# A hybrid decoder block on one Trainium2 core: the last key and query sums of each recurrence half placed behind the newest bank add on VectorE

## The chip, the core and the metric

The kernel runs on one core of a Trainium2 chip. Five engines work side by side, each on its own list of instructions in program order: TensorE (PE in the profile; its weight loads are PEld), VectorE (DVE), ScalarE (ACT), GpSimd (POOL) and SyncE (SP), which issues most of the transfers. They wait for each other through semaphores. Matmuls write into PSUM, here eight banks of 128 x 512 fp32 values; the other engines read a bank out, or add it onto a tile in SBUF.

The metric is the device time of one execution in microseconds. The kernel before took 1442.57 us (median of three runs, 1440.68 to 1442.67).

## The reference, cut to what matters

```
proj = x @ w_in -> [q | f | i | og | pool_v | gate_a | gate_b]
a = HGRN2(q, f, i) -> per-head RMSNorm * sigmoid(og) -> @ w_a
b = per-group linear(causal_mean_w(pool_v) - pool_v) * pool_scale
mix = (sigmoid(gate_a) * a + sigmoid(gate_b) * b) @ w_out
x = LN(alpha * x + mix);  x = LN(alpha * x + relu(x @ w_up)^2 @ w_down)

# HGRN2, per head, in chunks:
G = cumsum(log_f);  q_dec = q * exp(G);  k_inv = k * exp(-G);  k_to_end = k * exp(G_last - G)
scores = tril(q_dec @ k_inv^T);  o = scores @ v + q_dec @ state
state  = exp(G_last) * state + k_to_end^T @ v
```

All of it is fp32, with 1024 tokens, a width of 1024, 8 heads of 128 and one layer. What the change touches lies in the HGRN2 part: the products of the keys and queries with their decays.

## The kernel before, in words

**The products.** Every fp32 operand is split into a rounded high part and the rest, and each block product is three matmuls of 128 x 512 (high by high, high by rest, rest by high: lines 213, 215 and 216 in `prod`). The products with `w_in` run by a seven-product scheme for 2 x 2 blocks: `pair` makes one such group of seven products of 12 matmuls each. A weight block becomes its two parts by a cast on ScalarE (line 250) and a subtraction on VectorE (line 251); the sums of weight blocks that the scheme needs are made on VectorE too (lines 303, 320, 328, 335).

**Bank adds.** The seven products of a group go into three PSUM banks. Where a bank holds a sum that belongs to two outputs, ScalarE copies it to a tile (`copied`, line 294) and VectorE later adds a bank onto that tile (`added`, line 298: the *bank add*, which writes a tile named `c` or `f`). In the order used through the recurrence (p1, p2, p6, p7, p5, p4, p3) the bank called `a` is read by the bank add after p5, and p3 goes on adding to the same bank. Between p5 and p3 stands one product on another bank, p4. So p3 cannot start before that bank add is done.

**The recurrence beside the products.** Each of the 8 heads is done in two halves of 512 tokens; this text numbers the halves 0 to 15. For each half `Half.prepare` makes the scaled keys and queries in pieces on VectorE, ScalarE and GpSimd; then come the transposes of `ke` (`turn_keys`, line 1069), the scores (line 1076), the states and the outputs. The pieces are run by `recurrence`, a generator; after each product of the projections (`run` and `run_ahead`) one step of it is taken, so the recurrence's work is spread between the products. Some 8.25 products go to one half.

The last two pieces of `prepare` make, for one half: `q` times a decay for odd blocks of 16 (line 1049), `kr` likewise for even blocks (line 1050; the tile is called `tE`), `ke` = `kr` times `ek` (line 1052; tile `tC`), and `q64` and `k64` for the far scores by 32 keys: of each, one half is copied on ScalarE (lines 1057, 1060) and the other multiplied on VectorE (lines 1058, 1061). Right after them `far_queries` makes `tA` from `q` (line 1096).

**What sets the order.** PE's order through this stage is as the program is written. On the other engines a scheduler with its own estimate of times sets the order at build time, within the dependences. `tc.issue_after(i)` is one more bound: what is written inside it stands behind instruction `i` on the same engine's list. It is no wait on a semaphore. The kernel uses it already as `behind_act`: the copies to `q64` and `k64` stand behind the newest ScalarE instruction of a product's result (`last_act`).

Names in the rows of the order: `tE` is `kr`, `tC` is `ke`, `tA` is `far_queries`' result or a running decay product, `raw` is a weight block or a sum of such, `w` a weight part, `pA` and `pC` are running sums of the causal pooling, `st` the state, `ps_pj` a bank of a projection product, `T` and `p32` decays.

Of the kernel before, what the change touches and what calls it, by code (L numbers as in the profile page):

```python
# [16 lines left out]
P = 128  # L17
# [6 lines left out]
CH = HALF // P  # L24
SUB = 16
NB = HALF // SUB
# [26 lines left out]
def tile_hybrid_block(  # L53
# [19 lines left out]
    V, A, G, PE = nc.vector, nc.scalar, nc.gpsimd, nc.tensor  # L73
# [16 lines left out]
    def nm(s):  # L90
        seq[0] += 1
        return f"{s}_{seq[0]}"
# [7 lines left out]
    def ps_tile(tag="pj", bufs=4):  # L100
        if tag == "hg":
            hg_tags.append(hg_tags.pop(0))
            tag, bufs = hg_tags[-1], 1
        return pp.tile([P, HALF], F32, tag=tag, name=nm("ps_" + tag), bufs=bufs)
# [76 lines left out]
    def minus_sum(out, a, b):  # L181
        V.scalar_tensor_tensor(out, a, -1.0, b, ALU.mult, ALU.subtract)
# [25 lines left out]
    def prod(ps, w, name, first):  # L208
        wh, wl = w
        for k in range(CH):  # L210
            th, tl = xp[name][k][:, 0], xp[name][k][:, 1]
            with tc.high_priority(PRIO_WHOLE) if k else nullcontext():
                PE.matmul(ps, wh[:, k], th, start=first and k == 0, stop=False, skip_group_check=True)  # L213
            with tc.high_priority(PRIO_WHOLE):
                PE.matmul(ps, wh[:, k], tl, start=False, stop=False, skip_group_check=True)  # L215
                PE.matmul(ps, wl[:, k], th, start=False, stop=k == CH - 1, skip_group_check=True)  # L216

    def block_tile(shape=(CH, P)):
        return wq.tile([P, *shape], F32, tag="raw", name=nm("raw"), bufs=6)
# [23 lines left out]
    def w_tile():  # L243
        return wq.tile([P, CH, P], F32R, tag="w", name=nm("w"), bufs=NW)

    hi_of, lo_of, last_act = [], [], [None]

    def w_part(src):
        hi, lo = w_tile(), w_tile()
        hi_of.append(A.copy(hi, src).ins)  # L250
        lo_of.append(V.tensor_sub(lo, src, f(hi)).ins)  # L251
        return hi, lo
# [7 lines left out]
    def noted(i):  # L260
        last_act[0] = i.ins
        return i

    def behind_act():
        return tc.issue_after(last_act[0])

    n_c = [0]

# [17 lines left out]
    def pair(raw, rooms, takes, pz_tag="pj", twin=False, pc_tag="pj", turned=False):  # L286


        b11, b12, b21, b22, t = raw if len(raw) == 5 else (*raw, None)
        c, ps = {}, {}  # L290

        def copied(room, ps):
            t = room()
            noted(A.copy(t, ps))  # L294
            return t

        def added(t, ps):
            V.tensor_add(t, t, ps)  # L298
            return t

        def make_t3():
            c["t"] = block_tile() if t is None else t
            V.tensor_sub(c["t"], b22, b12)  # L303

        def t3():
            if twin:
                make_t3()
            return w_part(c["t"])

        def t2():  # L310
            if not twin:
                make_t3()
                make_t2()
            return w_part(b12)

        def make_t2():
            if turned:
                minus_sum(b12, c["t"], b11)
            else:
                V.tensor_add(b12, c["t"], b11)  # L320

        def t4():
            if twin:
                make_t2()
            if turned:
                minus_sum(b21, b12, b21)
            else:
                V.tensor_sub(b21, b21, b12)
            return w_part(b21)

        def t1():
            if turned:
                minus_sum(c["t"], b22, b12)
            else:
                V.tensor_sub(c["t"], b22, b12)
            return w_part(c["t"])

        def p1(w):
            ps["a"] = ps_tile()
            prod(ps["a"], w, "a11", True)  # L340
            c[11] = copied(rooms[0], ps["a"])

        def p2(w):
            if pz_tag == "pj":
                ps["z"] = ps_tile()
            ps["c"] = ps_tile(pc_tag, 4 if pc_tag == "pj" else 2)
            prod(ps["c"], w, "a12", True)

        def p7(w):
            if pz_tag != "pj":  # L350
                ps["z"] = ps_tile(pz_tag, 2)
            prod(ps["z"], w, "s3", True)
            with tc.high_priority(PRIO):
                takes[0](added(c[11], ps["c"]))
                c[22] = copied(rooms[2], ps["z"])

        def p6(w):
            prod(ps["a"], w, "s2", False)
            with tc.high_priority(PRIO):
                c[21] = copied(rooms[1], ps["a"])  # L360
                if twin:
                    takes[2](added(c[21], ps["z"]))

        def p4(w):
            prod(ps["z"], w, "a22", False)
            if not twin:
                with tc.high_priority(PRIO):
                    takes[2](added(c[21], ps["z"]))

        def p5(w):  # L370
            prod(ps["a"], w, "s1", False)
            with tc.high_priority(PRIO):
                takes[3](added(c[22], ps["a"]))

        def p3(w):
            prod(ps["a"], w, "s4", False)
            with tc.high_priority(PRIO):
                takes[1](ps["a"])

        def t0():  # L380
            return w_part(b11)

        def b_21():
            return w_part(b21)

        def b_22():
            return w_part(b22)

        middle = (
            ((t3, p7), (t4, p4), (t2, p6), (t1, p5)) if twin else ((t2, p6), (t3, p7), (t1, p5), (t4, p4))  # L390
        )
        return tuple(
            ((operand,), ((operand, product),)) for operand, product in ((t0, p1), (b_21, p2), *middle, (b_22, p3))
        )
# [66 lines left out]
    with tc.tile_pool(name="xr", bufs=8, side="right", reuse_waits="tile") as xr:  # L461
# [5 lines left out]
        ps = ps_tile("hg", 2)  # L467
# [274 lines left out]
    with tc.tile_pool(name="tmp", bufs=1, side="right", reuse_waits="tile") as tmp:  # L742
# [15 lines left out]
        def tt(tag, dtype=F32):  # L758
            pool = tmp if tag in ("q", "f", "og", "v") else hgp
            return pool.tile([P, HALF], dtype, tag=tag, name=nm(tag), bufs=RINGS.get(tag, 1))  # L760

        def small(tag, shape, bufs=2):
            n = math.prod(shape[1:])
            t = hgp.tile([P, max(n, LINE)], F32, tag=tag, name=nm(tag), bufs=bufs)[:, :n]
            return t if len(shape) == 2 else t.rearrange("p (a b) -> p a b", b=shape[2])
# [204 lines left out]
        def pairs_of(t):  # L970
            return t.rearrange("p (b e s) -> p b e s", e=2, s=SUB)

        def half64(t, e):
            return t.rearrange("p (c e b s) -> p c e b s", e=2, b=2, s=2 * SUB)[:, :, e]

        def bc(a, shape):
            return a.unsqueeze(len(a.shape)).to_broadcast(shape)
# [4 lines left out]
        def b32(t):  # L982
            return t.rearrange("p (b s) -> p b s", s=32)

        class Half:
# [4 lines left out]
            def prepare(self):  # L990

                h, u = self.h, self.u
                ft, q = inputs[h][0][u], inputs[h][1][u]
# [4 lines left out]
                to_end = tt("tC")  # L998
# [14 lines left out]
                T2 = T.rearrange("p (b e) -> p b e", e=2)  # L1013
                p32 = small("p32", [P, CH, 4])
# [12 lines left out]
                ek = small("ek", [P, CH, 4])  # L1027
# [7 lines left out]
                with behind_act():  # L1035
                    A.activation(k, ft, AF.Identity, bias=cmask[:, P - 1 : P], scale=-1.0)
# [4 lines left out]
                with behind_act():  # L1041
                    A.copy(pairs_of(kc)[:, :, 0], pairs_of(kr)[:, :, 0])
                V.tensor_mul(pairs_of(kc)[:, :, 1], pairs_of(kr)[:, :, 1], bc(rT2[:, :, 1], [P, NB // 2, SUB]))
                self.qc = qc = tt("tF")
                with behind_act():
                    A.copy(pairs_of(qc)[:, :, 1], pairs_of(q)[:, :, 1])
                V.tensor_mul(pairs_of(qc)[:, :, 0], pairs_of(q)[:, :, 0], bc(rT2[:, :, 0], [P, NB // 2, SUB]))
                yield
                V.tensor_mul(pairs_of(q)[:, :, 1], pairs_of(q)[:, :, 1], bc(T2[:, :, 0], [P, NB // 2, SUB]))
                V.tensor_mul(pairs_of(kr)[:, :, 0], pairs_of(kr)[:, :, 0], bc(T2[:, :, 1], [P, NB // 2, SUB]))  # L1050
                self.ke = ke = to_end
                V.tensor_mul(b32(ke), b32(kr), bc(ek.rearrange("p c b -> p (c b)"), [P, 16, 32]))
                yield
                self.q64 = q64 = hgp.tile([P, CH, 2, 32], F32, tag="q64", name=nm("q64"))
                self.k64 = k64 = hgp.tile([P, CH, 2, 32], F32, tag="k64", name=nm("k64"))
                with behind_act():
                    A.copy(q64[:, :, 0], half64(q, 1)[:, :, 0])
                V.tensor_mul(q64[:, :, 1], half64(q, 1)[:, :, 1], bc(p32[:, :, 2], [P, CH, 32]))
                with behind_act():
                    A.copy(k64[:, :, 1], half64(kr, 0)[:, :, 1])  # L1060
                V.tensor_mul(k64[:, :, 0], half64(kr, 0)[:, :, 0], bc(p32[:, :, 1], [P, CH, 32]))
                self.q = q

            def turn_keys(self):
# [521 lines left out]
    for b in range(NBLK):  # L1586
# [3 lines left out]
        if last:  # L1590

            for ring in (dh, dw):
                t = fw.tile([P, M, 2, HALF], F32R, tag="draw", name=nm("dx"), bufs=2)
                ring[:0] = [(t[:, n], t[:, n + 1]) for n in (0, 2)]
        for i, (name, slot, chain, fresh, (u, nh)) in enumerate(steps):
# [13 lines left out]
            for c in range(CH):  # L1609
                t = u * CH + c  # L1610
# [10 lines left out]
    for i, c in ((0, 0), (0, 1), (1, 0), (1, 1), (0, 2), (1, 2), (0, 3), (1, 3)):  # L1621
        _, _, chain, fresh, (_, nh) = ends[i]
        ps = down_tile(ops[i], chain, fresh, c)
# [36 lines left out]
```

## Time and profile before

| | |
|---|---|
| median of three runs | 1442.57 us (1440.68, 1442.57, 1442.67) |
| time of the profiled execution | 1440.68 us |
| its span, first to last instruction | 1439.0 us |
| busy: PE, DVE, ACT, POOL | 1424.9, 1099.3, 753.6, 108.6 us |
| mean granted TensorE clock | 0.998 |
| recurrence beside the projections | about 113 to 546 us of the span |

A row of the timeline gives the start in us, the duration in us, engine, line, operation, output and inputs, the shape, and in brackets the idle time of the engine before it with what ended it. Instructions of VectorE and ScalarE overlap a little at their ends, so what an instruction takes of its engine is the distance from its start to the next start. Matmuls overlap by almost half; there too the distance of starts counts. A row of a table by stretches gives the stretch, its length, the busy time (and count) of PE, PEld, DVE, ACT and POOL, the granted clock, the transfer engines' share and GB/s.

### The profile page before, as it was taken

How to read it: one execution, taken by the hardware profiler on the slowest of the kernel's cores; microseconds unless marked ns; L12 is line 12 of the kernel's file. 1: busy time of each engine (PE TensorE's matmuls, PEld its weight loads, DVE VectorE, ACT ScalarE, POOL GpSimd, SP SyncE). 2: the span in 40 equal slices, each digit the busy share in tenths (PEclk: the TensorE clock that was granted, in tenths of full speed). 3: DMA queues.
4: the chain of work that ended last, by engine and by line, in shares of the span. 5: the costliest groups of instructions: out<-in, count | busy, mean ns of one | idle time of the engine just before them, and what ended most of it. 6: DMA issues, size and time to landing. Idle time of an engine off the chain costs nothing.

```text
span 1439.0 us, 21137 instructions
## 1 busy us (share of the span) xinstructions
PE 1424.9 (99%) x7499; PEld 1184.6 (82%) x7499; DVE 1099.3 (76%) x1816; ACT 753.6 (52%) x1376; POOL 108.6 (8%) x296
## 2 busy tenths in 40 slices
PE   9999999999999999999999999999999999999997
PEld 7888888888888888878888888888888888888886
DVE  5967887897797796579965697666666787777978
ACT  5445566666656655456532375555556443433534
POOL 0002011111211210100003000000000100000000
PEclk9999999999999999999999999999999999999999
DMA  7142254444454546799651225444456864444422
GB/s 271 62 137 91 87 131 148 109 128 145 110 125 132 142 124 189 214 325 348 190 205 64 99 66 189 155 161 161 149 180 245 292 243 146 149 141 167 133 73 117
DMA packets 186794, 228.17 MB, mean 159 GB/s; under 512 B 12192, under 2 KB 110784, under 8 KB 186688
## 3 DMA queue, kind: packets, MB, share of 16 engines
q1 hardware_dynamic: 180080, 210.94, 44.0%
q0 software_dynamic: 5824, 13.63, 4.5%
q10 hardware_dynamic: 784, 2.25, 0.5%
q8 instruction: 59, 0.97, 0.3%
q14 instruction: 47, 0.39, 0.1%
HBM read 149.70 MB, written 77.07 MB: 158 GB/s over the span
## 4 chain that ended last, share of the span: by engine, by line
PE 94%; DVE 3%; DMA 1%; issue 1%; ACT 1%; DVEq 0%; POOL 0%; ACTq 0%; SPq 0%; POOLq 0%
PE ps_pj L213 16%; PE ps_pj L215 16%; PE ps_pj L216 16%; PE ps_pj L1539 4%; PE ps_pj L1538 4%; PE ps_pj L1537 4%; PE ps_pj L115 2%; PE ps_pj L116 2%; PE ps_pj L114 2%; PE ps_tr L1539 2%; PE ps_tr L1538 2%; PE ps_tr L1537 2%; PE ps_hg L216 1%; PE ps_sc L213 1%; PE ps_sc L216 1%; PE ps_hg L213 1%
## 5 line engine op out<-in xcount | busy, mean ns | idle before, releaser
L213 PE MATMUL ps_pj<-act,w 128*128 128x512 f32 x1068 | 420.1, 393 | 2.7 <-DVE c L298 2.4
L215 PE MATMUL ps_pj<-act,w 128*128 128x512 f32 x1068 | 415.4, 389 | 0.0
L216 PE MATMUL ps_pj<-act,w 128*128 128x512 f32 x1068 | 415.1, 389 | 0.0
L250 ACT CAST w<-raw 128x512 fp32r<-128x512 f32 x303 | 187.7, 621 | 260.6 <-PE ps_pj L215 179.9
L251 DVE TENSOR_TENSOR w<-raw,w 128x512 fp32r<-128x512 f32 x303 | 207.1, 686 | 95.8 <-ACT w L250 93.3
L213 PEld LDWEIGHTS ps_pj<-act,w 128*128 128x128 f32 x1068 | 200.6, 188 | 46.1 <-DVE c L298 3.7
L216 PEld LDWEIGHTS ps_pj<-act,w 128*128 128x128 f32 x1068 | 200.5, 188 | 42.2
L215 PEld LDWEIGHTS ps_pj<-act,w 128*128 128x128 f32 x1068 | 200.6, 188 | 40.4
L1499 ACT CAST act<-act 128x1024 fp32r<-128x1024 f32 x66 | 67.1, 1050 | 108.4 <-issue 35.0
L1538 PE MATMUL ps_pj<-act,act 128*128 128x512 f32 x240 | 93.1, 389 | 0.0
L1539 PE MATMUL ps_pj<-act,act 128*128 128x512 f32 x240 | 93.1, 389 | 0.0
L1500 DVE TENSOR_TENSOR act<-act,act 128x1024 fp32r<-128x1024 f32 x66 | 79.4, 1219 | 17.4 <-ACT act L1499 17.4
L1537 PE MATMUL ps_pj<-act,act 128*128 128x512 f32 x240 | 92.6, 389 | 0.0
L298 DVE TENSOR_TENSOR c<-c,ps_pj 128x512 f32<-128x512 f32 x91 | 62.1, 683 | 33.4 <-PE ps_pj L216 32.3
L294 ACT COPY c<-ps_pj 128x512 f32<-128x512 f32 x92 | 53.3, 581 | 3.3 <-PE ps_pj L216 1.8
L1538 PEld LDWEIGHTS ps_pj<-act,act 128*128 128x128 f32 x240 | 45.1, 188 | 9.5 <-DVE act L1500 0.2
L1537 PEld LDWEIGHTS ps_pj<-act,act 128*128 128x128 f32 x240 | 45.1, 188 | 9.4
L1539 PEld LDWEIGHTS ps_pj<-act,act 128*128 128x128 f32 x240 | 45.1, 188 | 9.3
L303 DVE TENSOR_TENSOR raw<-raw,raw 128x512 f32<-128x512 f32 x43 | 29.6, 688 | 24.6 <-DMA raw<-in_w_in_dram 19.7
L1408 ACT ACTIVATE c<-c 128x512 f32<-128x512 f32 x61 | 38.5, 633 | 1.7
L1407 ACT ACTIVATE c<-c 128x512 f32<-128x512 f32 x46 | 29.0, 632 | 16.3 <-DVE c L298 16.3
L737 POOL DMA_DIRECT2D s<-og x28 | 24.9, 1162 | 137.1 <-DVE og L1150 137.1
(432 smaller groups left out, 2706.4 us busy)
## 6 DMA issues: line engine op xcount, KB each, us to landing
h<-c SPq DMA_DIRECT2D x106, 256.0 KB, 2.9
raw<-in_w_in_dram SPq DMA_DIRECT2D x100, 256.0 KB, 3.3
act<-h SPq DMA_DIRECT2D x78, 256.0 KB, 2.9
draw<-in_w_down_dram SPq DMA_DIRECT2D x16, 1024.0 KB, 8.2
raw<-in_w_up_dram SPq DMA_DIRECT2D x56, 256.0 KB, 2.9
hf<-h SPq DMA_DIRECT2D x34, 256.0 KB, 2.9
s<-og POOLq DMA_DIRECT2D x28, 256.0 KB, 6.0
v<-v SPq DMA_DIRECT2D x16, 256.0 KB, 3.4
```

The source lines that it names most:

```text
L213: PE.matmul(ps, wh[:, k], th, start=first and k == 0, stop=False, skip_group_check=True)
L215: PE.matmul(ps, wh[:, k], tl, start=False, stop=False, skip_group_check=True)
L216: PE.matmul(ps, wl[:, k], th, start=False, stop=k == CH - 1, skip_group_check=True)
L250: hi_of.append(A.copy(hi, src).ins)
L251: lo_of.append(V.tensor_sub(lo, src, f(hi)).ins)
L294: noted(A.copy(t, ps))
L298: V.tensor_add(t, t, ps)
L1499: A.copy(hi, src)
L1500: V.tensor_sub(lo, src, f(hi))
L1537: PE.matmul(ps, hh[:, w], wh, start=fresh and n == 0, stop=False, skip_group_check=True)
L1538: PE.matmul(ps, hh[:, w], wl, start=False, stop=False, skip_group_check=True)
L1539: PE.matmul(ps, hl[:, w], wh, start=False, stop=n == M - 1, skip_group_check=True)
```

## The change

`added` now notes its bank add in `last_add`, and `behind_add` places what is written inside it behind the newest bank add. The last VectorE products of `prepare` stand inside it: lines 1049, 1050 and 1052 in one piece, lines 1058 and 1061 in the next. The two ScalarE copies stand together. What is computed, and the count of instructions, stay the same. The line numbers behind line 246 move by 3, and from here on by 4 to 5 behind the changed piece.

```diff
-    hi_of, lo_of, last_act = [], [], [None]
+    hi_of, lo_of, last_act, last_add = [], [], [None], [None]
...
+    def behind_add():
+        return tc.issue_after(last_add[0])
...
         def added(t, ps):
-            V.tensor_add(t, t, ps)
+            last_add[0] = V.tensor_add(t, t, ps).ins
             return t
...
-                V.tensor_mul(pairs_of(q)[:, :, 1], pairs_of(q)[:, :, 1], bc(T2[:, :, 0], [P, NB // 2, SUB]))
-                V.tensor_mul(pairs_of(kr)[:, :, 0], pairs_of(kr)[:, :, 0], bc(T2[:, :, 1], [P, NB // 2, SUB]))
-                self.ke = ke = to_end
-                V.tensor_mul(b32(ke), b32(kr), bc(ek.rearrange("p c b -> p (c b)"), [P, 16, 32]))
+                with behind_add():
+                    V.tensor_mul(pairs_of(q)[:, :, 1], pairs_of(q)[:, :, 1], bc(T2[:, :, 0], [P, NB // 2, SUB]))
+                    V.tensor_mul(pairs_of(kr)[:, :, 0], pairs_of(kr)[:, :, 0], bc(T2[:, :, 1], [P, NB // 2, SUB]))
+                    self.ke = ke = to_end
+                    V.tensor_mul(b32(ke), b32(kr), bc(ek.rearrange("p c b -> p (c b)"), [P, 16, 32]))
                 yield
...
                 with behind_act():
                     A.copy(q64[:, :, 0], half64(q, 1)[:, :, 0])
-                V.tensor_mul(q64[:, :, 1], half64(q, 1)[:, :, 1], bc(p32[:, :, 2], [P, CH, 32]))
-                with behind_act():
                     A.copy(k64[:, :, 1], half64(kr, 0)[:, :, 1])
-                V.tensor_mul(k64[:, :, 0], half64(kr, 0)[:, :, 0], bc(p32[:, :, 1], [P, CH, 32]))
+                with behind_add():
+                    V.tensor_mul(q64[:, :, 1], half64(q, 1)[:, :, 1], bc(p32[:, :, 2], [P, CH, 32]))
+                    V.tensor_mul(k64[:, :, 0], half64(kr, 0)[:, :, 0], bc(p32[:, :, 1], [P, CH, 32]))
```

PE's list is the same before and after. On VectorE the order moves in halves 0, 3, 4, 6, 8, 9, 10, 14 and 15, and in the other seven it stays; ScalarE, GpSimd and SyncE each swap a few neighbours. Three places on VectorE follow.

Half 10 on VectorE, before: the bank add `c_795` reads bank `ps_pj_766` after p5.

```order
L917 TENSOR_TENSOR pC_793_4423<-pA_792_4421 128x269
L1050 TENSOR_TENSOR tE_779_4356<-tE_779_4356,T_769_4316 128x16x16
L328 TENSOR_TENSOR raw_811_4501<-raw_811_4501,raw_813_4504 128x512
L1049 TENSOR_TENSOR q_737_4142<-q_737_4142,T_769_4316 128x16x16
L917 TENSOR_TENSOR pA_794_4425<-pC_793_4423 128x265
L1052 TENSOR_TENSOR tC_763_4291<-tE_779_4356,ek_774_4329 128x512
L1061 TENSOR_TENSOR k64_809_4494<-tE_779_4356,p32_770_4318 128x4x32
L298 TENSOR_TENSOR c_795_4431<-c_795_4431,ps_pj_766_4297 128x512
L1058 TENSOR_TENSOR q64_808_4493<-q_737_4142,p32_770_4318 128x4x32
```

The same place after.

```order
L920 TENSOR_TENSOR pC_793_4423<-pA_792_4421 128x269
L331 TENSOR_TENSOR raw_811_4501<-raw_811_4501,raw_813_4504 128x512
L920 TENSOR_TENSOR pA_794_4425<-pC_793_4423 128x265
L301 TENSOR_TENSOR c_795_4431<-c_795_4431,ps_pj_766_4297 128x512
L1053 TENSOR_TENSOR q_737_4142<-q_737_4142,T_769_4316 128x16x16
L925 TENSOR_TENSOR pA_794_4425<-pA_794_4425,inv_n_86 128x7
L927 SCALAR_TENSOR_TENSOR c_767_4310<-pA_794_4425,c_767_4310 128x249
L1054 TENSOR_TENSOR tE_779_4356<-tE_779_4356,T_769_4316 128x16x16
```

Four products (`tE`, `q`, `tC`, `k64`) that stood ahead of the bank add now stand behind it; `q64` and `k64` stand behind the next bank add, `c_782`, further down.

Half 15 on VectorE, before: the bank add `c_1131` reads bank `ps_pj_1108` after p5.

```order
L1050 TENSOR_TENSOR tE_1121_6026<-tE_1121_6026,T_1111_5986 128x16x16
L1049 TENSOR_TENSOR q_969_5323<-q_969_5323,T_1111_5986 128x16x16
L328 TENSOR_TENSOR raw_1141_6146<-raw_1141_6146,raw_1143_6149 128x512
L922 TENSOR_TENSOR pC_1094_5927<-pC_1094_5927,inv_n_86 128x15
L924 SCALAR_TENSOR_TENSOR c_1086_5908<-pC_1094_5927,c_1086_5908 128x241
L917 TENSOR_TENSOR pA_1095_5933<-c_1058_5761 128x271
L1052 TENSOR_TENSOR tC_1105_5961<-tE_1121_6026,ek_1116_5999 128x512
L298 TENSOR_TENSOR c_1131_6088<-c_1131_6088,ps_pj_1108_5967 128x512
L1061 TENSOR_TENSOR k64_1139_6139<-tE_1121_6026,p32_1112_5988 128x4x32
L1058 TENSOR_TENSOR q64_1138_6138<-q_969_5323,p32_1112_5988 128x4x32
```

The same place after, down to the sums `q64` and `k64`.

```order
L331 TENSOR_TENSOR raw_1141_6146<-raw_1141_6146,raw_1143_6149 128x512
L925 TENSOR_TENSOR pC_1094_5927<-pC_1094_5927,inv_n_86 128x15
L927 SCALAR_TENSOR_TENSOR c_1086_5908<-pC_1094_5927,c_1086_5908 128x241
L920 TENSOR_TENSOR pA_1095_5933<-c_1058_5761 128x271
L926 TENSOR_TENSOR c_1086_5908<-pC_1094_5927,c_1086_5908 128x15
L301 TENSOR_TENSOR c_1131_6088<-c_1131_6088,ps_pj_1108_5967 128x512
L1053 TENSOR_TENSOR q_969_5323<-q_969_5323,T_1111_5986 128x16x16
L1054 TENSOR_TENSOR tE_1121_6026<-tE_1121_6026,T_1111_5986 128x16x16
L251 TENSOR_TENSOR w_1160_6257<-raw_1143_6149,w_1159_6256 128x512
L920 TENSOR_TENSOR pC_1096_5935<-pA_1095_5933 128x269
L1100 TENSOR_TENSOR tA_1158_6248<-q_969_5323,eq_1115_5994 128x512
L1056 TENSOR_TENSOR tC_1105_5961<-tE_1121_6026,ek_1116_5999 128x512
```

`tE`, `q` and `tC` moved from ahead of the bank add to behind it, and the small `c_1086` product of 15 columns moved ahead of it. Behind these rows come the bank add `c_1124`, then `q64` and `k64`.

Earlier in half 15 on VectorE, before: the sum of weight blocks `raw_1142`, which needs a block that a transfer brings.

```order
L303 TENSOR_TENSOR raw_1142_6148<-raw_1144_6151,raw_1143_6149 128x512
L924 SCALAR_TENSOR_TENSOR c_1047_5715<-pC_1072_5820,c_1047_5715 128x256
L917 TENSOR_TENSOR pA_1087_5912<-c_1086_5908 128x271
L1038 TENSOR_TENSOR tE_1121_6026<-f_954_5251,tC_1105_5961 128x512
L320 TENSOR_TENSOR raw_1143_6149<-raw_1142_6148,raw_1140_6144 128x512
```

The same place after.

```order
L927 SCALAR_TENSOR_TENSOR c_1047_5715<-pC_1072_5820,c_1047_5715 128x256
L920 TENSOR_TENSOR pA_1087_5912<-c_1086_5908 128x271
L306 TENSOR_TENSOR raw_1142_6148<-raw_1144_6151,raw_1143_6149 128x512
L1041 TENSOR_TENSOR tE_1121_6026<-f_954_5251,tC_1105_5961 128x512
L920 TENSOR_TENSOR pC_1088_5914<-pA_1087_5912 128x269
```

Two pooling steps (`c_1047`, `pA_1087`) moved from behind `raw_1142` to ahead of it.

In half 4 the bank add `c_433` (bank `ps_pj_410`) stood behind `tE`, `q`, `tC` and `k64` and now follows the block sum `raw_443` at once; in half 6 the add `c_523` moved ahead of `q`, `tE` and `tC` in the same way. In half 0 only `q` (line 1049) moved from ahead of the bank add `c_195` to behind it.

## The prediction

> **What bounds the kernel now.** I read the page first, then the table by stretches, TensorE's waits, and the timelines of TensorE and VectorE around them.
>
> From the page, the span and the group of bank adds:
>
> ```profile
> span 1439.0 us, 21137 instructions
> ...
> L298 DVE TENSOR_TENSOR c<-c,ps_pj 128x512 f32<-128x512 f32 x91 | 62.1, 683 | 33.4 <-PE ps_pj L216 32.3
> ```
>
> From the table by stretches: VectorE's dense stretch, and the recurrence stage.
>
> ```profile
> 386.00:435.00 49.00, 48.05 (x296) 40.06 (x295) 48.52 (x110) 28.40 (x65) 11.24 (x29) 1.00 0.43 108
> 113.00:546.00 433.00, 430.54 (x3012) 362.25 (x3014) 359.68 (x738) 263.30 (x590) 79.14 (x235) 1.00 0.45 125
> ```
>
> From TensorE's waits (total us, times, longest):
>
> ```profile
> PE ps_pj L213 <- DVE c L298: 2.4, 2, 1.4
> ...
> PE ps_tr L114 <- DVE f L891: 0.7, 1, 0.7
> ```
>
> TensorE is the bound: in the stage that the change touches it lacks work for 433.00 - 430.54 = 2.46 us. So an edit on VectorE can win only these 2.46 us and what a restart costs, while it can lose without such a limit. Nearly all of the 2.46 is two waits, both for a bank add. Here they are in TensorE's timeline, with the starts of the products around them, and a third, short one:
>
> ```profile
> 127.48 0.39 PE L216 MATMUL ps_pj<-act,w 128*128 128x512 f32 x1
> 127.95 0.50 PE L213 MATMUL ps_pj<-act,w 128*128 128x512 f32 x1
> ...
> 397.84 0.39 PE L213 MATMUL ps_pj<-act,w 128*128 128x512 f32 x1
> ...
> 400.34 0.39 PE L216 MATMUL ps_pj<-act,w 128*128 128x512 f32 x1
> 401.67 0.50 PE L213 MATMUL ps_pj<-act,w 128*128 128x512 f32 x1 [0.94 <-DVE c L298]
> ...
> 404.56 0.38 PE L1126 MATMUL ps_hg<-v,att 128*128 128x128 f32 x2
> ...
> 539.17 0.39 PE L216 MATMUL ps_pj<-act,w 128*128 128x512 f32 x1
> 541.00 0.50 PE L213 MATMUL ps_pj<-act,w 128*128 128x512 f32 x1 [1.44 <-DVE c L298]
> ...
> 543.85 0.38 PE L1126 MATMUL ps_hg<-v,att 128*128 128x128 f32 x2
> ...
> 546.10 0.25 PE L1076 MATMUL sc<-q,k 128*32 128x64 f32 x2
> ```
>
> Undisturbed, eleven steps take 400.34 - 397.84 = 2.50 us, so a step is 0.227 and a product of 12 is 2.73. Starts tell the true cost of a wait: at half 10, 401.67 - 400.34 - 0.23 = 1.10 us, and the product that follows takes 404.56 - 401.67 = 2.89, 0.16 over. At half 15 it is 541.00 - 539.17 - 0.23 = 1.60 us and 2.85, 0.12 over. At half 0 it is 127.95 - 127.48 - 0.23 = 0.24 us; a restart cost of 0.14 there is an estimate, the mean of the other two.
>
> All three are p3 waiting for the bank add that reads p5's bank.
>
> **The change part by part.** No instruction is added or removed, and TensorE's list is the same. So each edit is worth what it does to one of these waits, less any wait that it makes.
>
> *Half 10.* VectorE's timeline ahead of the late bank add:
>
> ```profile
> 398.52 0.41 DVE L1050 TENSOR_TENSOR tE<-tE,T 128x256 f32<-128x256 f32 x1
> 398.85 0.68 DVE L328 TENSOR_TENSOR raw<-raw,raw 128x512 f32<-128x512 f32 x1
> 399.45 0.41 DVE L1049 TENSOR_TENSOR q<-q,T 128x256 f32<-128x256 f32 x1
> 399.79 0.42 DVE L917 TENSOR_TENSOR pA<-pC 128x265 f32<-128x265 f32 x1
> 400.14 0.68 DVE L1052 TENSOR_TENSOR tC<-tE,ek 128x512 f32<-128x512 f32 x1
> 400.74 0.28 DVE L1061 TENSOR_TENSOR k<-tE,p 128x128 f32<-128x128 f32 x1
> 400.94 0.67 DVE L298 TENSOR_TENSOR c<-c,ps_pj 128x512 f32<-128x512 f32 x1
> ```
>
> By distance of starts, L1050 takes 0.33, L1049 0.34, L1052 0.60 and L1061 0.20: together 1.47 us that now stand behind the add. It starts at 400.94 - 1.47 = 399.47 and ends at 400.14. TensorE resumes 0.06 after an add's end (401.61 to 401.67), so it may go on at 400.20, while it would come there at 400.34 + 0.23 = 400.57. p5's bank is full by 397.84 or a little later, so the add itself does not wait. The wait goes: 1.10 + 0.16 = 1.26 us.
>
> *Half 0.* L1049 alone leaves (0.34), more than the 0.24 lost: 0.24 + 0.14 = 0.38 us.
>
> *Half 15.* Three places of VectorE's timeline:
>
> ```profile
> 528.01 0.69 DVE L303 TENSOR_TENSOR raw<-raw,raw 128x512 f32<-128x512 f32 x1 [1.22 <-DMA raw<-in_w_in_dram]
> 528.62 0.42 DVE L924 SCALAR_TENSOR_TENSOR c<-pC,c 128x256 f32<-128x256 f32 x1
> 528.95 0.43 DVE L917 TENSOR_TENSOR pA<-c 128x271 f32<-128x271 f32 x1
> 529.30 0.68 DVE L1038 TENSOR_TENSOR tE<-f,tC 128x512 f32<-128x512 f32 x1
> ...
> 540.27 0.68 DVE L298 TENSOR_TENSOR c<-c,ps_pj 128x512 f32<-128x512 f32 x1
> ...
> 542.47 0.16 DVE L923 TENSOR_TENSOR c<-pC,c 128x15 f32<-128x15 f32 x1
> 542.56 0.67 DVE L298 TENSOR_TENSOR c<-c,ps_pj 128x512 f32<-128x512 f32 x1
> ```
>
> L1050, L1049 and L1052 leave the add's front (0.33 + 0.34 + 0.60 = 1.27, by the distances of half 10), L923 enters it (0.09): the add comes 1.18 earlier. That alone leaves 1.60 - 1.18 = 0.42 us of wait and the restart cost. But 12 us before, L924 and L917 (529.30 - 528.62 = 0.68 us) now run while VectorE idles 1.22 us for a transfer, so all behind them comes 0.68 earlier. Together 1.86, more than 1.60: the wait goes, with 0.26 us to spare. I take this: 1.60 + 0.12 = 1.72 us. The other end is 1.18.
>
> *The other halves.* In halves 3, 8, 9 and 14 only the far sums pass a bank add, and no wait of TensorE lies there; halves 4 and 6 are a rival below. I price these at nothing; the cover is the distance to the scores.
>
> *What is late next.* The far scores of half 15 need the copies on ScalarE, which follow the add at 542.56:
>
> ```profile
> 543.99 0.29 ACT L1060 COPY k<-tE 128x128 f32<-128x128 f32 x1
> ```
>
> The copies end at 544.28, the far scores start at 546.10: 1.82 us. TensorE will be 1.72 earlier here. The add at 542.56 moves up too: ahead of it nothing is new but the 0.68 that fell into the idle time, and the far sums `k64` and `q64` (two of 0.20) fell behind it while the pooling step of 0.35 came ahead. So it and the copies are some 0.7 earlier, and 0.8 us is left.
>
> After half 10 the danger is VectorE's own pace. It is busy for 48.52 of 49.00 us from 386 to 435, so it does not move up when TensorE does. The next add of this kind, and the product that needs it:
>
> ```profile
> 423.67 0.68 DVE L298 TENSOR_TENSOR f<-f,ps_pj 128x512 f32<-128x512 f32 x1
> ```
>
> ```profile
> 425.78 0.39 PE L213 MATMUL ps_pj<-act,w 128*128 128x512 f32 x1
> ```
>
> It allows TensorE to go on at 424.35 + 0.06 = 424.41; TensorE will come at 425.78 - 1.26 = 424.52. That holds by 0.1 us. Elsewhere the page's group of bank adds shows VectorE idle for 32.3 us in front of 91 adds until TensorE is done, so the two engines fall back into step.
>
> ScalarE's and SyncE's swaps are of neighbours; the weight parts are used some 10 us after they are made. I price them at nothing.
>
> **The sum.** 1.26 + 0.38 + 1.72 = 3.36 us. The profiled execution took 1440.68 (span 1439.0 and 1.7 around it), so its like would take 1437.3. That execution was the fastest of the three; the same gain from the median, 1442.57, gives 1439.2, or 0.23% less. About 0.2%, 2.9 us, is what a measurement of this kernel can tell from no change.
>
> **The rivals.**
>
> *A part of the wait stays.* If the 0.68 at half 15 is not won (the transfer lands later) the gain is 1.18 there; if the 0.1 at 424 fails by some 0.3, that and a restart of 0.14 go too. 3.36 - 0.54 - 0.44 = 2.4, or 2.8 with the first alone: 1439.8 to 1440.2. For it speak the two thin margins, 0.26 and 0.1.
>
> *VectorE stands idle behind the add.* In half 4 the add now stands where L1050 stood, at 236.06, yet p5's last matmul runs until 236.58 + 0.39 = 236.97:
>
> ```profile
> 236.06 0.42 DVE L1050 TENSOR_TENSOR tE<-tE,T 128x256 f32<-128x256 f32 x1
> ```
>
> ```profile
> 236.58 0.39 PE L216 MATMUL ps_pj<-act,w 128*128 128x512 f32 x1
> ```
>
> So VectorE loses 0.91 us there, and by estimate as much in half 6. If all of it came through to TensorE, the gain would be 3.36 - 1.82 = 1.5: 1441.0. Against it: half 4's scores are 8 us away, and the idle in front of bank adds takes such a delay up. [...]
>
> *The gain is waited away later.* From 590 to 640 the products of the pooling run beside many transfers, and TensorE waits 0.7 us there for L891. If transfers set that stage's clock, TensorE comes 3.36 earlier and waits that much more: 1442.6. Against it: these transfers are issued when tiles come free, which TensorE paces.
>
> *Slower: the far sums come too late for the scores.* In nine halves the last sums move behind an add, and the scores of 32 keys wait on them. If TensorE stands there by x in each, the time changes by 9x - 3.36: it decides from x = 0.37 us, and x = 1 gives 1448.2. Against it: the distance of 0.8 us that is left at half 15, the nearest that I found.
>
> **How the numbers follow.** Forecast 0.55, part stays 0.18, idle VectorE 0.07, waited away 0.07, slower 0.13. The time is that of the first, 1439.2. The range goes down by the spread of the three runs below their median (1.9) to 1437.2, and up to the cases of no gain and 1 us of noise, 1443.6; what is left out is most of the slower case. The forecast lies only 0.5 us beyond the 2.9, so about seven tenths of it and a third of the second fall under "faster", with a little of the rest: 0.47; most of the slower case is over 0.2%: 0.12; the rest, 0.41, is within.
>
> **What would show it.** Right: no wait of L213 for L298, and the recurrence stage's lack of work under 0.5 us in place of 2.46; the bank add of half 10 ahead of L1053 (1049 before), and TensorE's steps of 0.227 running through. Wrong: a wait of L1080 (the scores) or L1073 (the transposes) for VectorE or ScalarE; a wait for the add near 424 or 541; a longer wait at L114. If TensorE's lack of work falls as said and the time does not, the restart costs and the noise of the runs are mis-sized.

## The result, and the profile after

The changed kernel took 1439.80 us (median of 20 runs, 1436.71 to 1442.90); the kernel before, beside it, 1442.19 us (20 runs, 1439.92 to 1446.37). The ratio is 0.9981 with an interval of 0.9974 to 0.9988: 2.4 us in the medians, 1.7 to 3.7 us by the interval. The profiled execution took 1439.73 us, its span is 1438.0.

TensorE's waits in it (total us, times, longest), and the recurrence stage in the table by stretches:

```profile
PE ps_hg L474 <- POOL inv_n L150: 1.7, 1, 1.7
PE sc L1080 <- ACT q L1061: 1.6, 1, 1.6
...
PE ps_tr L114 <- DVE f L894: 0.5, 1, 0.5
```

```profile
113.00:546.00 433.00, 431.42 (x3047) 363.59 (x3049) 359.58 (x739) 262.77 (x594) 79.31 (x235) 1.00 0.45 124
```

The line "L213 <- DVE c" with its 2.4 us is gone, so none of the three waits for the bank add is left. In its place stands a wait that the profile before did not have: the scores (L1080) wait 1.58 us for ScalarE's copy of `q64`. All of the 433.00 - 431.42 = 1.58 us that TensorE now lacks in this stage is that one wait.

VectorE's timeline at half 10 shows the bank add where the order had it, ahead of `q`, `tE` and `tC`:

```profile
397.93 0.42 DVE L920 TENSOR_TENSOR pA<-pC 128x265 f32<-128x265 f32 x1
398.28 0.67 DVE L301 TENSOR_TENSOR c<-c,ps_pj 128x512 f32<-128x512 f32 x1
398.88 0.41 DVE L1053 TENSOR_TENSOR q<-q,T 128x256 f32<-128x256 f32 x1
```

And TensorE's timeline at halves 0, 10 and 15, where p3 follows p4:

```profile
126.66 0.39 PE L216 MATMUL ps_pj<-act,w 128*128 128x512 f32 x1
126.89 0.40 PE L213 MATMUL ps_pj<-act,w 128*128 128x512 f32 x1
...
399.18 0.39 PE L216 MATMUL ps_pj<-act,w 128*128 128x512 f32 x1
399.41 0.39 PE L213 MATMUL ps_pj<-act,w 128*128 128x512 f32 x1
...
540.27 0.39 PE L216 MATMUL ps_pj<-act,w 128*128 128x512 f32 x1
540.50 0.39 PE L213 MATMUL ps_pj<-act,w 128*128 128x512 f32 x1
```

At all three places the step is 0.23 us. Half 13 in TensorE's timeline, and the same place in the table by stretches (the number behind the five engines is the granted clock):

```profile
486.26 0.46 PE L1080 MATMUL sc<-tF,tD 128*32 128x32 f32 x32
488.29 0.44 PE L1080 MATMUL sc<-q,k 128*32 128x64 f32 x3 [1.58 <-ACT q L1061]
...
489.68 0.63 PE L215 MATMUL ps_pj<-act,w 128*128 128x512 f32 x1
490.11 0.63 PE L216 MATMUL ps_pj<-act,w 128*128 128x512 f32 x1
...
492.24 0.63 PE L215 MATMUL ps_pj<-act,w 128*128 128x512 f32 x1
```

```profile
487.00:489.40 2.40, 1.11 (x33) 1.00 (x34) 1.80 (x4) 2.40 (x8) 0.13 (x2) 1.00 0.43 133
489.40:492.80 3.40, 3.40 (x9) 2.66 (x9) 3.37 (x7) 3.04 (x12) 1.02 (x2) 0.50 0.75 219
```

The wait is only half of the price: right behind it the clock is 0.50 for 3.4 us, and a matmul takes 0.43 us (490.11 - 489.68) instead of 0.23. By the starts of the same instructions in both profiles the whole event costs TensorE 3.5 us.

Put together, the time of TensorE's instruction after less before, by their starts:

| from | to | moves by, us |
|---|---|---|
| start of the kernel | 113 us (transfers at the start, no part of the change) | -0.8 |
| half 0 | the product p3 | -0.37 |
| half 10 | the product p3 | -1.27 |
| half 13 | scores and the products at half clock | +3.5 |
| half 15 | the product p3 | -1.73 |
| L114, 622 to 630 us | its waits for L894 | -0.35 |
| sum | | -1.0 |

So the change did at its three places what was forecast, 3.4 us, and one event at a fourth place took as much back in this execution. What that event is, is the question of the experiments.

This is where VectorE stands in half 13: first the kernel before, then the changed one.

```profile
482.50 0.69 DVE L303 TENSOR_TENSOR raw<-raw,raw 128x512 f32<-128x512 f32 x1 [2.67 <-DMA raw<-in_w_in_dram]
```

```profile
483.02 0.69 DVE L306 TENSOR_TENSOR raw<-raw,raw 128x512 f32<-128x512 f32 x1 [5.58 <-DMA raw<-in_w_in_dram]
```

VectorE's order is the same here in both kernels. It waits for one weight block, and everything to the copy of `q64` is queued behind that. SyncE's timeline in the changed kernel shows what goes out just ahead of the block (the last row):

```profile
472.52 0.37 SPq L224 DMA_DIRECT2D raw<-in_w_in_dram  x1
472.95 1.07 SPq L887 DMA_DIRECT2D f<-gb  x2
474.34 0.32 SPq L736 DMA_DIRECT2D o<-og  x1
474.94 0.38 SPq L224 DMA_DIRECT2D raw<-in_w_in_dram  x1
```

Two loads of the pooling's gates (`f<-gb`), which are not used before 590 us, stand ahead of it, and GpSimd sends three accumulating transfers of 256 KB at the same time:

```profile
474.62 2.66 POOL L740 DMA_DIRECT2D s<-og  x3 [7.43 <-DVE og L1154]
```
The block landed 8.0 us after its issue; in the profile before, among the same transfers, 5.4 us. The two gate loads go out 1.99 and 1.26 us ahead of the block and the three accumulating ones from 0.33 us ahead of it to 0.80 us behind it, in both profiles alike.

### The profile page after: what moved, and what is told of

Its sections match the earlier page's. It is cut to its first block, busy times and chain, and to the rows that moved or that the text cites. A ratio compares the mean times of both kernels' runs of the same rounds, so it can differ in the third digit from the quotient of the medians.

```text
span 1438.0 us, 21148 instructions
## 1 busy us (share of the span) xinstructions
PE 1425.0 (99%) x7499; PEld 1184.9 (82%) x7499; DVE 1099.5 (76%) x1816; ACT 753.0 (52%) x1376; POOL 108.7 (8%) x296
## 4 chain that ended last, share of the span: by engine, by line
PE 96%; DMA 2%; ACT 1%; DVE 1%; issue 0%; POOL 0%; DVEq 0%; SPq 0%; ACTq 0%; POOLq 0%
PE ps_pj L213 16%; PE ps_pj L215 16%; PE ps_pj L216 16%; PE ps_pj L1543 4%; PE ps_pj L1541 4%; PE ps_pj L1542 4%; PE ps_pj L114 2%; PE ps_pj L116 2%; PE ps_pj L115 2%; PE ps_tr L1543 2%; PE ps_tr L1541 2%; PE ps_tr L1542 2%; PE ps_hg L215 1%; PE ps_sc L215 1%; PE ps_sc L213 1%; PE ps_hg L213 1%
## 5 line engine op out<-in xcount | busy, mean ns | idle before, releaser
L213 PE MATMUL ps_pj<-act,w 128*128 128x512 f32 x1068 | 420.4, 394 | 0.2 <-ACT c L297 0.2
L213 PEld LDWEIGHTS ps_pj<-act,w 128*128 128x128 f32 x1068 | 200.9, 188 | 43.0 <-ACT c L297 1.3
L1503 ACT CAST act<-act 128x1024 fp32r<-128x1024 f32 x66 | 66.9, 1050 | 110.1 <-issue 35.0
L306 DVE TENSOR_TENSOR raw<-raw,raw 128x512 f32<-128x512 f32 x43 | 29.6, 689 | 28.3 <-DMA raw<-in_w_in_dram 24.8
```

## The experiments

**The changed kernel again.** No edit.

> The changed kernel once more. In its first profile TensorE waited 1.58 us in half 13 (scores, for ScalarE's copy of q64), and then 8 products ran at half the clock: together about 3.4 us, which eats nearly all that was won. The transfer of a weight block took 8.0 us from issue to landing there, 5.4 in the kernel before, at the same place among the same transfers. Theory A, chance: the block's transfer races with three accumulating transfers of GpSimd's queue, and which wins differs from execution to execution, in both kernels alike. Then the landing time and the wait differ in this profile; where the wait is absent, TensorE's lack of work from 113 to 546 us is under 0.5 us and the span is about 1434.6. Rival B, the change causes it: the wait is there again, 1.3 to 1.8 us, with a landing of 7.5 to 8.5 us. Both: median 1439 to 1441, no wait of a product for the bank add.

Measured: 1439.83 us (ratio 0.9985, 0.9976 to 0.9994). The block landed after 7.2 us and the scores waited 0.89 us; the mean granted clock of the execution was 0.999, in the first profile 0.998. No wait for the bank add at halves 0, 10 and 15. In half 13, where none was expected, p3 waits 0.24 us for its bank add; the profiles of the kernel before show below where that comes from. So the event comes again, with another size; B is not excluded by this run alone.

**Only the first piece behind the add.**

```diff
-                    A.copy(k64[:, :, 1], half64(kr, 0)[:, :, 1])
-                with behind_add():
-                    V.tensor_mul(q64[:, :, 1], ...)
-                    V.tensor_mul(k64[:, :, 0], ...)
+                V.tensor_mul(q64[:, :, 1], ...)
+                with behind_act():
+                    A.copy(k64[:, :, 1], half64(kr, 0)[:, :, 1])
+                V.tensor_mul(k64[:, :, 0], ...)
```

> Only the first piece (q, tE, tC) stands behind the bank add; q64 and k64 with their copies as in the kernel before. Theory: the waits are what the first piece's own 0.33 + 0.34 + 0.60 us ahead of the add cost. Half 10 and half 0 as in the full change (1.2 and 0.38 us won). In half 15 the add comes 1.27 us earlier and not more, since the two pooling steps don't move into the idle time ahead of it: a wait of about 0.2 to 0.4 us stays. Together 2.9 us, so 0.4 us less than the full change, before whatever half 13 does. Rival: the far sums carry part of it; then a wait of over 0.5 us stays in half 10 or the gain is under 2 us in the profile's waits.

Measured: 1439.51 us (0.9982, 0.9973 to 0.9991). No wait at halves 0 and 10; at half 15 this stays:

```profile
539.09 0.39 PE L216 MATMUL ps_pj<-act,w 128*128 128x512 f32 x1
539.64 0.50 PE L213 MATMUL ps_pj<-act,w 128*128 128x512 f32 x1 [0.17 <-DVE c L301]
```

By the starts it is 539.64 - 539.09 - 0.23 = 0.32 us, within the 0.2 to 0.4 expected (0.17 us of it is idle time): the three products of the first piece carry all of the effect at halves 0 and 10, and most of it at half 15. In half 13 the scores waited 1.1 us here too, and p3 0.26 us.

**Only the far sums behind the add.**

```diff
-                with behind_add():
-                    V.tensor_mul(pairs_of(q)[:, :, 1], ...)
-                    V.tensor_mul(pairs_of(kr)[:, :, 0], ...)
-                    self.ke = ke = to_end
-                    V.tensor_mul(b32(ke), b32(kr), ...)
+                V.tensor_mul(pairs_of(q)[:, :, 1], ...)
+                V.tensor_mul(pairs_of(kr)[:, :, 0], ...)
+                self.ke = ke = to_end
+                V.tensor_mul(b32(ke), b32(kr), ...)
```

> Only the far sums (q64, k64) stand behind the bank add, their copies together; q, tE and tC as in the kernel before. Theory: half 0 as before (0.24 us lost), half 10 wins only the 0.20 us of k64 (a wait of about 0.75 us stays of 0.94), half 15 wins the 0.68 us of the two pooling steps that fill the idle time (a wait of about 0.75 us stays of 1.44). Together 0.9 us: median about 1441.3. Rival, my prediction's slower case: the far sums come too late for the scores, with waits of the scores for VectorE or ScalarE in several of the nine halves and a time above the kernel before.

Measured: 1440.36 us (0.9989, 0.9981 to 0.9998), 0.9 us below the median expected. TensorE's timeline at halves 10 and 15:

```profile
401.13 0.50 PE L213 MATMUL ps_pj<-act,w 128*128 128x512 f32 x1 [0.74 <-DVE c L301]
...
540.47 0.39 PE L216 MATMUL ps_pj<-act,w 128*128 128x512 f32 x1
541.11 0.50 PE L213 MATMUL ps_pj<-act,w 128*128 128x512 f32 x1 [0.26 <-DVE c L301]
```

Half 10 is as worked out, to 0.01 us. Half 15 was expected to keep 0.75 us and keeps 0.26: the weight block that VectorE waits for there landed 0.50 us earlier against TensorE's p3 than in the kernel before (p3's undisturbed start less the start of L303 or L306: 540.47 + 0.23 - 528.81 = 11.89 us, before 539.17 + 0.23 - 528.01 = 11.39), which is the whole difference. In half 13 the scores waited 1.0 us and p3 0.28 us; in none of the nine halves whose order moves did the scores wait. So the far sums do not come too late, and this part alone gains a little.

**Three places against one transfer: the gate loads later.** The order of all engines but SyncE stays that of the changed kernel.

```diff
+    block_loads = []
...
         done = nc.sync.dma_start(out=t, in_=rows_of[:, :, c : c + t.shape[2]])
+        block_loads.append(done.ins)
...
-                        nc.sync.dma_start(out=t, in_=gbd[j][u])
+                        with tc.issue_after(block_loads[81]):
+                            nc.sync.dma_start(out=t, in_=gbd[j][u])
```

> The full change, and the first three loads of the pooling's gates (256 KB each) stand some 30 us later on SyncE, behind a later weight block. Two of them went out just ahead of the weight block of half 13 that came late. Theory A: with 512 KB less in front of it the block lands in 4 to 5 us instead of 5.4 to 8.0, VectorE's idle time ahead of L306 falls below 3 us, and the scores of half 13 do not wait in any execution. The profile's span is about 1434.6, and the median falls by the share of executions that had the wait times 3.4 us: 1437 to 1439. Rival: the accumulating transfers alone make it late; it lands in over 6.4 us, the wait stays, and the time is the changed kernel's within 0.5 us.

Measured: 1437.90 us (0.9973, 0.9964 to 0.9982). The stage in the table by stretches, and VectorE's wait for the block:

```profile
113.00:546.00 433.00, 433.00 (x3065) 364.93 (x3064) 361.89 (x745) 265.86 (x598) 79.78 (x235) 1.00 0.45 126
```

```profile
480.41 0.69 DVE L309 TENSOR_TENSOR raw<-raw,raw 128x512 f32<-128x512 f32 x1 [1.43 <-DMA raw<-in_w_in_dram]
```

The block landed after 4.2 us, and TensorE never waits in these 433 us. The span, 1436.2, is longer than the 1434.6 expected; 1.2 of these 1.6 us were lost, against the first profile of the change, in the first 7 us of the execution, among the first transfers.

**The kernel before, two more profiles.** No edit.

> The kernel before, unchanged, for one more profile. The four kernels with part or all of the change and the gate loads in their old place all show the wait of half 13 (0.9 to 1.6 us); the one profile of the kernel before does not. Theory A, chance: the block's landing differs from execution to execution in this kernel too, and where it takes over 6.4 us (5.4 plus the 1.0 us that the copies ended ahead of the scores) the scores wait; the first profile, at 1440.7 us the quickest of its three runs and 1.5 below the median of twenty, would be one of the better executions. Then this profile, or the second, shows a landing over 6.4 us and a wait of the scores, and a span of 1440 to 1442. Theory B, the change makes the block late: landing 5 to 6 us and no wait of the scores here, in both profiles.

> As the run before it: the kernel before, unchanged, a second further profile. Chance: at least one of the two with the block landing in over 6.4 us and a wait of the scores. The change as cause: 5 to 6 us and no such wait in both.

Measured: 1441.70 and 1443.07 us. In the first the block landed after 6.1 us and the scores did not wait. In the second, after 7.6 us, they did. TensorE's waits in the second:

```profile
PE ps_pj L213 <- DVE c L298: 2.8, 3, 1.6
...
PE ps_tr L114 <- DVE f L891: 1.5, 1, 1.5
PE sc L1076 <- ACT q L1057: 0.9, 1, 0.9
```

The three waits for the bank add in this list are not those of the prediction: half 10, half 15, and one in half 13 that the first profile of before does not have. Both further profiles have it, the first of them too, where the scores did not wait:

```profile
495.45 0.50 PE L213 MATMUL ps_pj<-act,w 128*128 128x512 f32 x1 [0.28 <-DVE c L298]
```

This add hangs on the same block. From the start of L303 to its start it takes 11.48, 11.47 and 11.48 us in the three profiles of before, so it comes as late as the block does. By the starts it costs TensorE 0.6 us, the slower start of the product included.

So the event belongs to the kernel before as well; the forecast was made on a profile that happened not to have it. Theory B falls.

**The kernel before with the gate loads later.** The edit of the gate loads above, on the kernel before.

> The kernel before with the gate loads alone moved to stand behind the later weight block; the key and query sums as they were. The move made the changed kernel 1.9 us quicker in the median (1439.8 to 1437.9). Theory A (the wait of half 13 falls on the kernel before as well): the same here, 1.5 to 2 us below the kernel before, about 1440.3, and the three waits for the bank add stay (0.24, 1.1 and 1.6 us of loss). Theory B (only the change makes the block late): within 0.7 us of the kernel before.

Measured: 1440.59 us (0.9991, 0.9982 to 1.0000). The block landed after 4.0 us, no wait of the scores, the waits for the bank add at halves 0, 10 and 15 in place, none in half 13: theory A.

**The accumulating transfers of that moment left out.**

```diff
-        for name in ONTO[right, u]:
+        for name in ONTO[right, u] if (h, u) != (5, 1) else ():
```

> The full change with the gate loads in their old place, and the three accumulating transfers of one output (head 5, second half; the ones that go out beside the late block) left out, so that the sums they feed are incomplete. If those transfers make the block late, it lands in 4 to 5.5 us and the scores of half 13 do not wait: span 1434 to 1435.5 for the profile. If the two gate loads alone do it, the landing stays over 6.4 us and the wait of 0.9 to 1.6 us stays.

Measured: 1438.49 us (0.9974, 0.9963 to 0.9985). This kernel leaves out three transfers, so the sums that they feed are incomplete and its time is short of their work. Its span, 1436.6 us, is above the 1434 to 1435.5 expected; 1.76 us of it is a wait at L114. With the gate loads in their old place the block landed after 3.9 us and the scores did not wait. So it takes both: without the gate loads or without the accumulations the block is there in about 4 us; with both it took 5.4 to 8.0.

| kernel | block's landing, us after issue | wait of the scores in half 13, us | wait of p3 in half 13, us |
|---|---|---|---|
| before, three profiles | 5.4, 6.1, 7.6 | 0, 0, 0.86 | 0, 0.28, 0.28 |
| changed, three profiles | 8.0, 7.2, 5.9 | 1.58, 0.89, 0 | 0, 0.24, 0.17 |
| first piece; far sums | 7.5; 7.5 | 1.09; 1.00 | 0.26; 0.28 |
| gate loads later: changed (twice), before (twice) | 4.2, 3.9, 4.0, 4.0 | none | none |
| accumulations left out | 3.9 | none | none |

In the first profile of before the copies ended 1.0 us ahead of the scores, so a landing of over 5.4 + 1.0 = 6.4 us should be the point where the scores wait. All rows obey that, though the 6.1 us of the kernel before stands at the edge: its last copy ended at 488.67 and the far scores began at 488.61. The bank add is hit sooner: p3 waits in every row of 5.9 us or more, except where the scores' wait and the half clock had already made TensorE later than the add (8.0 us).

In all eight profiles that have both kinds of transfers, these go out at the same distances from the block, within 0.02 us. So what spreads the landing from 5.4 to 8.0 us is not the order or the time of their issue; what it is, is not shown.

**All of it once more, on one chip.** The changed kernel, and both kernels with the gate loads later.

> The changed kernel a third time, beside the kernels below on one chip. The block of half 13 lands in 5 to 8 us by chance; over 6.4 us the scores wait. Median 1439 to 1440.5, 0.1 to 0.25% under the kernel before; no wait of a product for the bank add at halves 0, 10 and 15.

> The full change with the gate loads later, a second time. With the race at half 13 gone, TensorE's three waits are all that separates it from the run below; by their starts they are worth 3.36 us (1.26 + 0.38 + 1.72). Median 1437 to 1438.5, no idle time of TensorE from 113 to 546 us. Rival: the change gives up part of the 3.36 us elsewhere (the pooling stage, L114); then the distance to the run below is under 2 us and L114's wait is longer here.

> The kernel before with the gate loads later, a second time: median 1440.2 to 1441.2, the three waits for the bank add in place, no wait of the scores.

Measured: 1438.80 us (0.9981, 0.9968 to 0.9993; a little under the range expected), 1437.69 us (0.9962, 0.9948 to 0.9976) and 1440.79 us (0.9982, 0.9973 to 0.9991). With the transfer out of the way the change is worth 1440.79 - 1437.69 = 3.1 us here, and 1440.59 - 1437.90 = 2.7 us in the earlier pair. The two spans, 1439.1 and 1435.8, differ by 3.3.

**Room for the pooling's gate loads.** The changed kernel with the gate loads later, and

```diff
-                    t = tt("v") if final else tt("f")
+                    t = tt("v") if final or (j, u) in ((2, 0), (3, 0)) else tt("f")
```

> The full change with the gate loads later, and two of the pooling's gate loads (of the groups 2 and 3, first half) in the two tiles of v that stand idle by then, so that the loads behind them need not wait for a tile of f. In the nine profiles so far TensorE waited 0.4 to 2.2 us at L114 from 620 to 633 us for VectorE's L894, which waited for such a load. If the tiles are what the loads lack, that wait goes and the median falls by 0.4 to 1.5 us, to 1436.5 to 1437.5. Rival: the transfers themselves set this stage's pace; the loads go out earlier, others land later, and the time stays within 0.4 us of the kernel with the gate loads later alone.

Measured: 1436.06 us (0.9952, 0.9938 to 0.9965), 1.6 us under the kernel with the gate loads later alone (1437.69) and 0.4 below the range expected; the block of half 13 landed after 4.1 us. TensorE's waits hold no L114 any more:

```profile
PE ps_hg L477 <- POOL inv_n L150: 1.7, 1, 1.7
PE ps_pj L213 <- ACT c L300: 0.8, 2, 0.6
PE ps_tr L171 <- DVE x L198: 0.7, 1, 0.7
```

The wait at L114, which added up to 0.4 to 1.8 us in all the other profiles, was for tiles, not for the transfers' pace: VectorE's order is the same here, and only the tiles of two loads and the times of the loads differ. A wait for ScalarE at 577 us, 0.6 us, is new. This is the quickest version here, 1442.78 - 1436.06 = 6.7 us under the kernel before in the medians; the change alone has 1442.78 - 1438.80 = 4.0 us beside it, the two edits of loads the other 2.7.

## Why the prediction was right, and where it was not

*Half 10.* 1.26 us worked out, 1.27 by the starts. The bank add has 399.41 - (398.28 + 0.67) - 0.06 = 0.40 us to spare, 0.37 by the prediction; 0.06 us is the time that it took TensorE to go on after an add's end.

*Half 0.* 0.38 worked out, 0.37 measured, the estimated restart cost of 0.14 included.

*Half 15.* 1.72 worked out, 1.73 measured, with 540.50 - (539.11 + 0.68) - 0.06 = 0.65 us to spare in place of 0.26:

```profile
528.74 0.69 DVE L306 TENSOR_TENSOR raw<-raw,raw 128x512 f32<-128x512 f32 x1 [0.52 <-DMA raw<-in_w_in_dram]
...
539.11 0.68 DVE L301 TENSOR_TENSOR c<-c,ps_pj 128x512 f32<-128x512 f32 x1
```

The two pooling steps went into the idle time as worked out: of 1.22 us, 0.52 are left. The rest of the room is the block, which landed 0.37 us earlier against TensorE (540.50 - 528.74 = 11.76 us in place of 11.39); why it did is not shown. The first piece alone, with the landing where it was in the kernel before, left 0.32 us, so that much of the 1.60 hung on the 0.68 us of the two pooling steps.

*The sum.* 3.36 us worked out; 3.1 and 2.7 us between medians with the transfer of half 13 out of the way, 2.4, 2.3 and 4.0 us with it, each uncertain by 1 to 2 us. The predicted 1439.2 us stands against 1439.8. Part of that closeness is luck: the median of three that the sum started from was 0.4 us above the median of twenty, from which the same sum gives 1442.19 - 3.36 = 1438.8, and the event of half 13 was not in it. The likeliest case came, and the numbers that carried it were starts of instructions, not counts of busy time.

*A part of the wait stays.* It did not, at the three places. The thin place near 424 us, 0.1 us by the prediction, held by 423.36 - (422.41 + 0.68) - 0.06 = 0.21 us:

```profile
422.41 0.68 DVE L301 TENSOR_TENSOR f<-f,ps_pj 128x512 f32<-128x512 f32 x1
```

```profile
423.36 0.40 PE L213 MATMUL ps_pj<-act,w 128*128 128x512 f32 x1
```

*VectorE stands idle behind the add.* It does, as worked out, 0.93 us in half 4 (0.91 predicted) and 0.77 us in half 6 (estimated at as much), and TensorE does not notice:

```profile
235.88 0.69 DVE L301 TENSOR_TENSOR c<-c,ps_pj 128x512 f32<-128x512 f32 x1 [0.93 <-PE ps_pj L216]
```

*The gain is waited away later.* Not seen. L114's waits were 0.7, 1.4 and 1.5 us in the kernel before, 0.5, 0.4 and 1.5 in the changed one; they scatter alike, and the spans above keep the whole 3.3 us.

*Slower: the far sums late for the scores.* Not so: no half but 13, whose order does not move, shows a wait of the scores, and the nearest of the others are the copies of half 15, 1.20 us ahead (0.8 predicted) and the sums of half 10, 1.81 us ahead.

*The step that was mis-sized* is "what is late next". It called 0.8 us at half 15 the nearest distance and looked only at halves whose order changes. In the very profile it used, half 13 had 1.00 us between the copies and the scores, and 495.29 - (493.98 + 0.68) - 0.06 = 0.57 us between the bank add and p3, and these are the distances that hang on a transfer. From ScalarE's, TensorE's and VectorE's timelines of the kernel before:

```profile
487.62 0.30 ACT L1060 COPY k<-tE 128x128 f32<-128x128 f32 x1
```

```profile
488.92 0.25 PE L1076 MATMUL sc<-q,k 128*32 128x64 f32 x2
...
495.29 0.39 PE L213 MATMUL ps_pj<-act,w 128*128 128x512 f32 x1
```

```profile
493.98 0.68 DVE L298 TENSOR_TENSOR c<-c,ps_pj 128x512 f32<-128x512 f32 x1
```

The sum should have had a term for it: about half a microsecond for p3 alone at a landing of 5.9 to 6.1 us; at a landing over 6.4 us, 1.8 us (the second further profile of before by the starts, 1.2 at the scores and 0.6 at p3) to 3.5 us (the profile after, with the clock), for kernels of either kind. It does not change the difference as long as both meet it equally often. The scores waited in two of three profiles of the changed kernel and in one of three of the kernel before, and a wait of either kind stands in three of three and two of three; whether the change makes it likelier stays open, since neither so few profiles nor the differences between medians can tell.

## What to carry to other kernels

Where a tight engine is full, an edit to its neighbours is worth the waits that it removes, read from the starts of instructions at each place and from the order of the instructions there; such a sum came out to a tenth of a microsecond at each of the three places here. Then look for the smallest distance between a result and its user over the whole stage, not only where the order changes, and above all for one that hangs on a transfer: one profile shows one draw of it (here 5.4 us in one and 7.6 us in another of the same kernel), and two or three profiles of the same kernel show whether it is luck. Loads that are needed a hundred microseconds later should not go out just ahead of one that is needed now: beside the same accumulations the block of half 13 took 5.4 to 8.0 us with the two gate loads ahead of it and 3.9 to 4.2 without.

## What was not expected of the hardware

*The clock.* In the first profile of the changed kernel a wait of 1.58 us between small matmuls (scores of 128x32 and 128x64) was followed by 3.4 us at a granted clock of 0.50. Waits of 0.86 to 1.09 us at the same place left no such stretch: in those four profiles p3, some 6 us behind the scores, still waited 0.24 to 0.28 us for its bank add, and 3.4 us at half the clock would have brought TensorE there 1.7 us later, behind the add. Nor did waits between dense products: behind 1.44 us at half 15 of the kernel before the granted clock was 1.00, and behind 1.76 us at L114 (the run without the accumulations) the steps were 0.23 us. Why this wait and not the others was not tried.

*The transfer.* One block of 256 KB took 5.4 to 8.0 us with the same neighbours in the queues, and 3.9 to 4.2 us with one kind of them out of the way. In the changed kernel's profile the transfer engines were busy throughout, while VectorE had nothing to do (the last two columns are their share and GB/s):

```profile
478.00:480.00 2.00, 2.00 (x11) 1.65 (x10) 0.00 (x0) 0.62 (x1) 0.00 (x0) 1.00 1.04 195
480.00:482.00 2.00, 2.00 (x10) 1.66 (x9) 0.00 (x0) 0.00 (x0) 0.00 (x0) 1.00 1.10 204
```

and the table of transfer queues from 477 to 484 us shows who held them:

```profile
q0 software_dynamic: 432, 0.79, 64.2%
q1 hardware_dynamic: 532, 0.31, 16.7%
```

GpSimd's 0.79 MB (the three accumulating transfers of 256 KB) took 64.2% of the transfer engines' time and SyncE's 0.31 MB 16.7%. SyncE's packets were the smaller ones, 0.31 MB in 532 against 0.79 MB in 432; in what order the transfer engines took up the two queues' packets is not shown here.
